# Hybrid decoder block: the gate projections as Strassen products, with sums of weights and tokens made in the first part

## The chip, the cores and the metric

The kernel runs on one core of a Trainium2 chip. The core has a matrix engine (TensorE, PE in the profile), three engines that work on tiles (VectorE or DVE, ScalarE or ACT, GpSimd or POOL), a queue engine that mainly issues transfers (SyncE, SP), and 16 DMA engines between DRAM and on-chip memory. Matmuls add up in PSUM banks of 128x512 float32. The metric is the device time of one execution in microseconds, the median of several runs.

## The reference, cut to what matters

```python
h = _rmsnorm(x, norm_pre_mix)              # x: (1, 2048, 1024)
proj = einsum('bsd,de->bse', h, w_in)
q, k, v = ...                              # 12 heads of 64, three dilations
u = gelu(proj[..., U0:Z0]); z = gelu(proj[..., Z0:GA0])   # 512 columns each
gate_a = sigmoid(proj[..., GA0:GB0])       # 1024 columns
gate_b = sigmoid(proj[..., GB0:IN_WIDTH])  # 1024 columns
y_attn = dilated attention of q, k, v
y_gmlp = u * (chunked spatial mix of layernorm(z))
merged = gate_a * (y_attn @ w_branch_attn) + gate_b * (y_gmlp @ w_branch_gmlp)
x = x + _rmsnorm(merged @ w_out)
h = _rmsnorm(x); x = x + _rmsnorm((relu(h @ w_mlp_in) ** 2) @ w_mlp_out)
```

The change concerns the products behind gate_a and gate_b: 2048 tokens by 1024 inputs by 2048 columns.

## The kernel before

Everything is float32, kept exact by splits: a number becomes a rounded high part and the rest as low part, and one product is three matmuls (high-high, high-low, low-high: `mm3`). `split_in` loads raw data, one engine makes the high part (L70 on ACT, L72 on POOL), another the low part by a subtraction (L78). Tokens are four chunks c of 512 in two halves (half 0: c = 0, 1). `hT[c]` is the normalised, transposed chunk, 8 slices of 128 inputs, both parts.

The program goes, for half 0 and then half 1, through v (`v_block`, eight blocks of 128 tokens) and q and k (`qk_pair`, twelve pairs per half: 48 matmuls, then DVE makes the rotation's products t, POOL joins them to r at L307 to L313, ACT and DVE split r into hl). Each half's weights wq come by `load_w`: 512 KB loads, high part on POOL, low part on DVE, three slots. While PE works on half 0, `keep_cols` also stores the transposed chunks 0 and 1 in DRAM (hT_d), because only two chunks fit on chip; chunks 2 and 3 stay on chip until the gates of half 1 are done, and `reload_h` brings 0 and 1 back one by one, high and low parts on POOL.

Then a generator, `filler`, works through u and z of half 1, the gates g of half 1 and half 0, and u and z of half 0. A step of it is one slice of one product, that is three matmuls. The attention is 48 units; between the pieces of a unit the program calls `steps(n)`, which puts n steps of the filler into PE's order, so that PE has work while ACT and DVE do the softmax. In PE's order of a unit there come: scores s, transposes pT of the previous unit's exponentials, products pv (from ph, a split made by ACT L688 and DVE L689, and pf, a copy by ACT L696), and transposes po of pvs (copied by ACT L704) whose reduction on DVE (L709) is the unit's output. Nine steps fall to a unit. After the units come `combine` (four chunks; att is stored, loaded back as A, weighted by DVE, and transposed to yt at L745, with fixed numbers of steps between) and the rest of the filler; then branches and gates are merged (from about 1104 us), and the MLP, which is itself made of Strassen products, follows.

The gates: 8 column blocks of 256 per half (w_g, `load_w`), each two column halves m by two chunks c by 8 slices: 96 matmuls. ACT copies each bank (gt) and SP stores it in gate_d. At sn == 6 of some of these products `sz_out` emits the spatial mixing of a z chunk.

PE's order is the order in which the program is written. ACT, DVE, POOL and SP are put in order by a scheduler, by its own model of when data will be there; on the chip each engine then runs its list strictly in that order, and an instruction that waits holds all behind it.

## Time and profile before

| what | value |
|---|---|
| runs | 2698.89, 2699.76, 2700.78 us; median 2699.76 |
| the profiled run | 2700.86 us, span 2698.8 us, granted clock 0.996 |
| v and qk, half 0 | 0 to 218 us |
| v and qk, half 1 | 218 to 425 us |
| u and z, half 1 | 425 to 514 us |
| gates of half 1 (hT_a), in the attention | 513.8 to 774.3 us |
| gates of half 0 (hT_b), attention and combine | 774.5 to 1013.6 us |
| u and z, half 0 | 1013.8 to 1104.2 us |

A profile row of instructions has line, engine, operation, tile names (out<-in), shapes and count, then busy time and the mean of one, then the time in which the engine sat idle before and what ended that. A row of the timeline has start and length in microseconds and, in brackets, the idle time before it. A row of a transfer has the tiles, the queue, count, KB each and the median time from issue to landing.

### The profile page before, as it was taken

How to read it: one execution, taken by the hardware profiler on the slowest of the kernel's cores; microseconds unless marked ns; L12 is line 12 of the kernel's file. 1: busy time of each engine (PE TensorE's matmuls, PEld its weight loads, DVE VectorE, ACT ScalarE, POOL GpSimd, SP SyncE). 2: the span in 40 equal slices, each digit the busy share in tenths (PEclk: the TensorE clock that was granted, in tenths of full speed). 3: DMA queues.
4: the chain of work that ended last, by engine and by line, in shares of the span. 5: the costliest groups of instructions: out<-in, count | busy, mean ns of one | idle time of the engine just before them, and what ended most of it. 6: DMA issues, size and time to landing. Idle time of an engine off the chain costs nothing. (4 is left out here: it accounts for less than half of the span.)

```text
span 2698.8 us, 34839 instructions
## 1 busy us (share of the span) xinstructions
PE 2663.4 (99%) x12674; PEld 2226.9 (83%) x12674; DVE 1582.5 (59%) x2677; ACT 1053.2 (39%) x2149; POOL 977.2 (36%) x837
## 2 busy tenths in 40 slices
PE   9999999999999999999899999999999999999998
PEld 8888888888888888888678888888888888888887
DVE  5665463334444345665456765555437888888866
ACT  5213111144444432344335555565545333333334
POOL 0351352210050004210413454323224776676645
PEclk9999999999999999999999999999999999999999
DMA  7445446266577846654656465554344212222236
GB/s 271 167 144 180 152 141 218 96 189 199 177 248 205 220 151 187 202 177 145 227 172 251 133 207 178 173 183 125 114 136 129 84 57 86 88 86 87 92 108 212
DMA packets 299197, 431.77 MB, mean 160 GB/s; under 512 B 52817, under 2 KB 166225, under 8 KB 299026
## 3 DMA queue, kind: packets, MB, share of 16 engines
q1 hardware_dynamic: 226864, 370.48, 43.5%
q10 hardware_dynamic: 64178, 32.06, 3.9%
q0 software_dynamic: 7984, 27.01, 2.6%
q8 instruction: 100, 1.64, 0.3%
q14 instruction: 71, 0.58, 0.1%
HBM read 286.67 MB, written 142.80 MB: 159 GB/s over the span
## 5 line engine op out<-in xcount | busy, mean ns | idle before, releaser
L1627 PE MATMUL ya<-T_spots,s 128*128 128x512 f32 x1176 | 289.4, 390 | 0.7 <-ACT T_spots L70 0.6
L1627 PEld LDWEIGHTS ya<-T_spots,s 128*128 128x128 f32 x1176 | 220.6, 188 | 47.4 <-ACT T_spots L70 1.0
L70 ACT ACTIVATE s<-sraw 128x768 fp32r<-128x768 f32 (+1 forms) x184 | 127.2, 696 | 330.4 <-POOL sraw L1428 155.7
L78 DVE TENSOR_TENSOR s<-sraw,s 128x512 fp32r<-128x512 f32 x172 | 184.1, 1095 | 8.6 <-ACT s L70 8.5
L1104 PE MATMUL aa<-B,A 128*128 128x512 f32 x768 | 182.3, 390 | 0.7 <-DVE A L85 0.7
L1104 PEld LDWEIGHTS aa<-B,A 128*128 128x128 f32 x768 | 143.9, 188 | 31.2 <-DVE A L85 1.1
L1627 PE MATMUL yc<-T_spots,s 128*128 128x512 f32 x624 | 159.7, 389 | 0.0
L72 POOL TENSOR_SCALAR w_g<-w_g_r 128x1024 fp32r<-128x1024 f32 x32 | 34.1, 1080 | 344.5 <-PE g L97 258.0
L1075 POOL TENSOR_TENSOR s<-w1r 128x512 f32<-128x512 f32 x32 | 42.3, 1322 | 309.3 <-DVE S L78 256.6
L95 PE MATMUL x<-hT_a,wq 128*128 128x512 f32 x384 | 149.8, 390 | 0.0
L96 PE MATMUL x<-hT_a,wq 128*128 128x512 f32 x384 | 149.5, 389 | 0.0
L97 PE MATMUL x<-hT_a,wq 128*128 128x512 f32 x384 | 149.5, 389 | 0.0
L709 DVE TENSOR_REDUCE o<-po 128x256 f32<-128x512 f32 x48 | 33.1, 690 | 184.3 <-PE po L708 184.3
L1627 PEld LDWEIGHTS yc<-T_spots,s 128*128 128x128 f32 x624 | 117.2, 188 | 24.3
L70 ACT ACTIVATE hl<-r 128x512 fp32r<-128x512 f32 x48 | 30.4, 632 | 238.1 <-POOL r L307 89.0
L95 PE MATMUL o<-wo,mg 128*128 128x512 f32 x256 | 102.1, 399 | 8.1 <-ACT mg L70 7.5
L78 POOL TENSOR_TENSOR T_spots<-w2r,T_spots 128x512 fp32r<-128x512 f32 x70 | 104.5, 1522 | 7.3 <-ACT T_spots L70 7.3
L95 PE MATMUL g<-hT_b,w_g 128*128 128x512 f32 x256 | 104.7, 409 | 0.0
L95 PE MATMUL g<-hT_a,w_g 128*128 128x512 f32 x256 | 104.3, 407 | 0.0
L78 DVE TENSOR_TENSOR A<-w1r,A 128x512 fp32r<-128x512 f32 x61 | 61.8, 1014 | 66.9 <-ACT A L70 66.9
L96 PE MATMUL o<-wo,mg 128*128 128x512 f32 x256 | 101.0, 394 | 0.0
L97 PE MATMUL o<-wo,mg 128*128 128x512 f32 x256 | 100.9, 394 | 0.0
(390 smaller groups left out, 7156.2 us busy)
## 6 DMA issues: line engine op xcount, KB each, us to landing
w1r<-in_w_mlp_in_dram SPq DMA_DIRECT2D x64, 512.0 KB, 3.8
sraw<-sd SPq DMA_DIRECT2D x128, 256.0 KB, 3.3
qk<-hl SPq DMA_DIRECT2D x24, 1024.0 KB, 5.1
qq<-qk SPq DMA_DIRECT2D x96, 256.0 KB, 4.9
w_g_r<-in_w_in_dram SPq DMA_DIRECT2D x32, 512.0 KB, 5.5
gated<-gt SPq DMA_DIRECT2D x64, 256.0 KB, 3.5
w2r<-in_w_mlp_out_dram SPq DMA_DIRECT2D x16, 1024.0 KB, 6.4
sd<-u ACTq DMA_DIRECT2D x63, 256.0 KB, 3.8
```

The source lines that it names most:

```text
L70: act.activation(hi, src, AF.Copy)
L72: pool.tensor_scalar(hi, src, 1.0, 1.0, op0=OP.mult, op1=OP.mult)
L78: (pool if lo_eng == "pool" else dve).tensor_sub(lo, src, f32(hi))
L95: pe.matmul(ps, lh, rh, start=start, stop=False)
L96: pe.matmul(ps, lh, rl, start=False, stop=False)
L97: pe.matmul(ps, ll, rh, start=False, stop=stop)
L709: dve.tensor_reduce(ot[:, :, j * 64:(j + 1) * 64], po.rearrange("p (b h e) -> p b e h", b=4, h=2), axis=AX.X, op=OP.add)
L1075: pool.tensor_add(s1, a21, a22)
L1104: pe.matmul(p, w[:, l, k, :], h[:, r, k, :], start=i in (1, 6, 5) and not k and not n, stop=k == 3 and n == 2, skip_group_check=True)
L1627: pe.matmul(p, s[:, l], w[r], start=i in (1, 2, 5) and not m and not o, stop=m == 1 and o == 2, skip_group_check=True)
```

## The change

Two neighbouring column halves (of 128) of a gate block, the two halves of the 1024 inputs and the two token chunks of a half form a 2x2 by 2x2 block product. Eight such pairs n per half are now done by Winograd's form of Strassen's scheme, seven products of 4 slices instead of eight: 12 matmuls each.

- In the first part, on POOL: `pre_s` (16 calls) loads a quarter of a block's weights and writes four sums of them to DRAM (sg_d, s1g_d); `pre_t` (16 calls) does the same for tokens (tg_d), whose four chunks are now all stored in hT_d by `keep_cols`. One call is written after each qk pair and after each v block of half 1; the scheduler is free in where it puts them.
- `gates()` takes the place of the 16 weight blocks. The products are grouped in phases: (1, 2), (6, 7), (5, 3), (4) for half 1, then the same for half 0; in a phase all eight n use the same one or two token operands. A product of one n is a piece: `piece` loads its weights (256 KB, rows of 512 bytes), `split_piece` splits them (POOL, DVE) into one of eight spots. The token operands of the next phase are loaded, as 512 KB loads, into opA or opB when the phase before has left it, and split by ACT and POOL (`operand`). Products of one n share banks and pass through 32 copies on ACT (L668, L670) and 80 additions on DVE (L673 to L684) into gx, gz and ga before the store.
- `reload_h` makes high parts on ACT instead of POOL. A unit of the attention has eight steps instead of nine, the combine's numbers of steps are 28, 18, 17, 19 instead of 33, 21, 20, 24, and u of half 0 runs chunk by chunk with both weight blocks held.

```diff
-            if c < 2:
-                raw = ...
+            raw = xp.tile([P, 4, P], F32, name=f"hr_{c}{i}{k}", tag="hr", bufs=3)
+            act.activation(raw, p3, AF.Copy)
+            sp.dma_start(hT_d[c, :, k:k + 4, i * P:(i + 1) * P], raw)
...
-            split_in(hT[c][:, :, k:k + 2], hT_d[c, :, k:k + 2, :], None, "pool", "pool")
+            split_in(hT[c][:, :, k:k + 2], hT_d[c, :, k:k + 2, :], None, "act", "pool")
...
+        def pre_t(half, k, j):
+            w = pre.tile([P, 5, 256], F32, name=f"pt{half}{k}{j}", tag="pre")
+            for c in range(2):
+                sp.dma_start(w[:, 2 * c:2 * c + 2], hT_d[2 * half + c][:, k::4, tsl])
+            b11, b21, b12, b22 = (w[:, n] for n in range(4))
+            pool.tensor_sub(b11, b12, b11)
+            pool.tensor_sub(b12, b22, b12)
+            pool.tensor_sub(b22, b22, b11)
+            pool.tensor_sub(b21, b21, b22)
+            pool.dma_start(tg_d[half][:, :, k, tsl], w[:, :4])
...
+        def pre_s(n, k):
+            sp.dma_start(both, a["w_in"][13 + n]...)
+            pool.tensor_add(s1, a21, a22)
+            pool.tensor_sub(a21, a11, a21)
+            pool.tensor_sub(a11, s1, a11)
+            pool.tensor_sub(a12, a12, a11)
+            pool.dma_start(sg_d[n]..., both)
+            pool.dma_start(s1g_d[n][:, k:k + 2], s1)
...
-    queue += [(13 + n, "g", n, 1) for n in range(8)] + [(13 + n, "g", n, 0) for n in range(8)]
+    queue += [(13, "g", 0, 1)]
...
+    PHASES = ((1, 2), (6, 7), (5, 3), (4,))
+    PIECES, SPLITS, LAST = 4, 3, 104
+    seq = [(half, i, n) for half in (1, 0) for ops in PHASES for i, n in lagged(ops)]
...
+    def operand(half, i, slot):
+        for k in range(0, 4, 2):
+            sp.dma_start(f32(slot)[:, 1, k:k + 2], src[i][:, k:k + 2])
...
+    def gates():
...
+        for t, (half, i, n) in enumerate(seq):
+            if t in starts:
...
+                    for j, i2 in enumerate(phases[ph + 1][1]):
+                        todo += operand(phases[ph + 1][0], i2, slots[s][:, j])
...
+            elif todo and (t % 2 == 0 or len(phases[ph][1]) == 1):
+                w, k = todo.pop(0)
+                split(w[:, 0, k:k + 2], w[:, 1, k:k + 2], f32(w)[:, 1, k:k + 2], "act", "pool")
+            piece(t + PIECES)
+            split_piece(t + SPLITS)
...
+            for k in range(4):
+                for m, (l, r) in enumerate(((0, 0), (0, 1), (1, 0))):
+                    pe.matmul(p, w[:, l, k], h[:, r, k], ...)
+                if t == 2 and late:
+                    sz_out(*late.pop(0))
+                yield
...
+            if i == 1:
+                act.activation(x, p, AF.Copy)
...
+            elif i == 6:
+                dve.tensor_add(z, x, p)
...
-    steps(6 if n > 1 else 9)
+    steps((6 if n < 4 else 5) if n > 1 else 9)
...
-        steps((33, 21, 20, 24)[n])
+        steps((28, 18, 17, 19)[n])
```

Three places in the engines' orders. The first is ACT in an attention unit. Before, each unit has the two ph, the exponentials e, pf and pvs, with a gate copy gt here and there:

```order
L688 ACTIVATE ph_4980<-pT_4975 128x512 [waits PE_49,Activation_49]
L663 ACTIVATE e_4946,o_4655<-e_4946,nm_4961 128x256 [waits DMAHW1_49,DVE_49]
L663 ACTIVATE e_4946,o_4655<-e_4946,nm_4961 128x256 x3
L688 ACTIVATE ph_4988<-pT_4983 128x256 [waits PE_49,Activation_49]
L696 ACTIVATE pf_4991<-pT_4983 128x256 [waits DVE_49]
L549 ACTIVATE gt_5008<-g_4933 128x512 [waits DMAHW6_49,PE_49]
L704 ACTIVATE pvs_5024<-pv_5015 128x512 [waits PE_49,Activation_49]
```

After (the names are the same; opB is the tile for token operands), at the end of the second phase:

```order
L833 ACTIVATE e_5521,o_5039<-e_5521,nm_5536 128x256 x3
L858 ACTIVATE ph_5563<-pT_5558 128x256 [waits PE_49,Activation_49]
L70 ACTIVATE opB<-opB 128x1024 [waits DMAHW1_49]
L866 ACTIVATE pf_5566<-pT_5558 128x256 [waits DVE_49]
L874 ACTIVATE pvs_5596<-pv_5587 128x512 [waits PE_49,Activation_49]
L70 ACTIVATE opB<-opB 128x1024 [waits DMAHW5_49]
```

PE's rows for the same stretch, after; g_5508 on its first row is the last product that reads the operand in opB's first half (g_5410 reads the second), and pf_5566 is used four rows on:

```order
L656 MATMUL g_5508<-opB,spots_4381 128x512 x3
L656 MATMUL g_5410<-opB,spots_4381 128x512 x12
L872 MATMUL pv_5587<-ph_5555,v_5038 128x256 x4
L872 MATMUL pv_5587<-ph_5563,v_5038 128x256 x2
L872 MATMUL pv_5587<-pf_5566,v_5038 128x128 x2
L656 MATMUL g_5508<-opB,spots_4381 128x512 x6
```

The two high parts of opB now stand ahead of pf_5566 and behind pvs_5596, each waiting for a transfer that the slot's last matmul lets go; ACT's list holds seven such places ahead of a pf.

The second is POOL in the first part. Before, the weights wq of the first qk pairs are its first work after the start:

```order
L72 TENSOR_SCALAR wq_941<-wq_r_942 128x1024
L72 TENSOR_SCALAR wq_941<-wq_r_946 128x1024
L72 TENSOR_SCALAR wq_952<-wq_r_953 128x1024
L72 TENSOR_SCALAR wq_952<-wq_r_957 128x1024
L72 TENSOR_SCALAR wq_1097<-wq_r_1098 128x1024
```

After (ps is the tile of a weight sum), the end of eleven calls of `pre_s`, which all stand ahead of the first wq:

```order
L442 DMA sgd<-ps_1755 256x1x512
L439 TENSOR_TENSOR ps_1858<-ps_1858 128x2x128
L443 DMA s1gd<-ps_1858 128x256
L440 TENSOR_TENSOR ps_1858<-ps_1858 128x2x128
L441 TENSOR_TENSOR ps_1858<-ps_1858 128x2x128
L442 DMA sgd<-ps_1858 256x1x512
L72 TENSOR_SCALAR wq_947<-wq_r_948 128x1024
L72 TENSOR_SCALAR wq_947<-wq_r_952 128x1024
L438 TENSOR_TENSOR ps_2087<-ps_2087 128x256
```

The high part of the first wq moved from the first place to the place behind eleven sums; one more weight sum and eight token sums follow at once.

The third is DVE at the turn from the last unit to the combine. Before, the last two reductions of po are followed by the low parts of w_u, and then by the combine's maximum M:

```order
L709 TENSOR_REDUCE o_8002<-po_8551 128x4x64 [waits PE_49]
L709 TENSOR_REDUCE o_8002<-po_8602 128x4x64 [waits PE_49]
L78 TENSOR_TENSOR w_u_8877<-w_u_r_8878,w_u_8877 128x1024 [waits DMAHW1_49,Pool_49]
L78 TENSOR_TENSOR w_u_8877<-w_u_r_8882,w_u_8877 128x1024 [waits DMAHW2_49,Pool_49]
L720 TENSOR_TENSOR M_8618<-A_8614 128x16 [waits DMAHW1_49,DMAHW0_49]
```

After (spots are the gate pieces, ga the adds of a gate's bank):

```order
L78 TENSOR_TENSOR spots_4165<-ga_4493,spots_4165 128x512 [waits DMAHW5_49,Pool_49]
L78 TENSOR_TENSOR w_u_9202<-w_u_r_9203,w_u_9202 128x1024 [waits DMAHW6_49,DMAHW3_49,DMAHW7_49,DMAHW1_49,Pool_49]
L879 TENSOR_REDUCE o_8413<-po_9048 128x4x64 [waits PE_49]
L684 TENSOR_TENSOR ga_4484<-ga_4484,g_9041 128x512 [waits PE_49]
L78 TENSOR_TENSOR w_u_9202<-w_u_r_9207,w_u_9202 128x1024 [waits DMAHW0_49,Pool_49]
```

The low part of the second w_u block moved ahead of the last reduction, and waits there for POOL's high part of it.

More of the change, by code (lines that the diff above doesn't have):

```diff
@@ L428, in block_kernel @@
                 v_block(rp, wv, c, i, between)
+                if half:
+                    next(pre_steps)()
                 if (c, i) == (0, 1):
@@ L521, in want, with lagged @@
             else:
-                loaded[q] = load_w(wi, f"w_{kind}{n}{half}", "pool" if (kind, half) == ("g", 0) and n == 2 else "dve")
+                loaded[q] = load_w(wi, f"w_{kind}{n}{half}")
+    PHASES = ((1, 2), (6, 7), (5, 3), (4,))
+    def lagged(ops):
+        first = [(n, (ops[0], n)) for n in range(8)]
+        return [z for _, z in sorted(first + [(n + 1.5, (i, n)) for n in range(8) for i in ops[1:]])]
+    PIECES, SPLITS, LAST = 4, 3, 104
+    seq = [(half, i, n) for half in (1, 0) for ops in PHASES for i, n in lagged(ops)]
@@ new lines, in block_kernel, with piece @@
+    g_ = dict(raw={}, w={}, b={})
+    def piece(t):
+        if t >= len(seq):
+            return
+        half, i, n = seq[t]
+        raws = g_["raws"]
+        r = raws[t % 4] if t < 8 else raws[4 + (t - LAST) % 5] if t >= LAST else raws[(t - 4) % 6]
+        if i < 3:
+            src = w_src(13 + n, i - 1)[:, :, :P]
+        elif i == 5:
+            src = s1g_d[n]
+        else:
+            kk, m = {6: (0, 0), 7: (0, 1), 3: (1, 0), 4: (1, 1)}[i]
+            src = sg_d[n][:, kk, :, m * P:(m + 1) * P]
+        sp.dma_start(r.rearrange("p (k c) -> p k c", k=4), src)
+        g_["raw"][t] = r
@@ L528, in filler @@
                 continue
+            if kind == "g":
+                yield from gates()
+                continue
             want(q)
-            want(q + 1)
-            if kind == "z" or (kind, n) == ("u", 1):
+            if queue[min(q + 1, len(queue) - 1)][1] != "g":
+                want(q + 1)
+            if (kind, n) == ("u", 1) or (kind, n, half) == ("u", 0, 0):
                 want(q + 2)
@@ L806, in block_kernel @@
     ec.close()
+    ega.close()
     e2r = ExitStack()
```

118 lines of the change are left out of this document (102 added, 16 removed).

## The prediction

> **What bounds the kernel now.** I read the page's totals first, then the windows by stage, then the rows of the gates, and last the timeline of one attention unit.
>
> ```profile
> span 2698.8 us, 34839 instructions
> PE 2663.4 (99%) x12674; PEld 2226.9 (83%) x12674; DVE 1582.5 (59%) x2677; ACT 1053.2 (39%) x2149; POOL 977.2 (36%) x837
> PEclk9999999999999999999999999999999999999999
> ...
> 87.00:218.00 131.00, 131.00 (x594) 108.80 (x593) 79.30 (x95) 17.01 (x29) 61.36 (x36) 1.00 0.53 166
> 514.00:720.00 206.00, 204.25 (x1167) 176.33 (x1166) 87.30 (x256) 85.49 (x252) 24.10 (x21) 1.00 0.64 196
> 720.00:940.00 220.00, 219.27 (x1250) 188.84 (x1249) 94.09 (x314) 94.75 (x297) 46.46 (x32) 1.00 0.76 214
> 940.00:1016.00 76.00, 76.00 (x393) 64.20 (x392) 30.32 (x109) 23.26 (x67) 8.10 (x9) 1.00 0.52 159
> ```
>
> A window row gives start and end, its length, then busy time and count of PE, PEld, DVE, ACT and POOL, the granted clock, the DMA share and GB/s. PE is busy for all but 35 us of 2698.8, at full clock in every slice. Two things therefore set the time: how many matmuls there are, and whether PE ever waits. Every removed matmul is a gain of one pitch; every microsecond in which PE must wait for another engine is a loss, because there is no idle PE time for it to vanish in. No other engine is above 45% in the stretch of the gates (514 to 1014), so it is late work, not too much work, that can hurt.
>
> **What is removed.** A row "a/b/c" gives shortest, median and longest ns.
>
> ```profile
> L95 PE MATMUL g<-hT_a,w_g x256: 388/390/487, 513.8 to 773.8; 128*128 128x512 f32 x128
> L97 PE MATMUL g<-hT_b,w_g x256: 388/391/398, 774.9 to 1013.6; 128*128 128x512 f32 x128
> ...
> L95 PE MATMUL x<-hT_a,wq 128*128 128x512 f32 x384 | 149.8, 390 | 0.0
> ...
> 142.69 4.27 POOL L309 TENSOR_TENSOR r<-t,t 128x512 f32<-128x512 f32 x2 [5.66 <-DVE t L304]
> 164.45 4.27 POOL L309 TENSOR_TENSOR r<-t,t 128x512 f32<-128x512 f32 x2 [3.93 <-DVE t L304]
> ```
>
> The gates are 2 x 3 x 256 = 1536 matmuls. After the change: 2 halves x 8 column blocks x 7 products x 4 slices x 3 terms = 1344, so 192 go. A matmul's 390 ns overlaps its neighbour's, so the price is the pitch: qk has 3 x 384 = 1152 matmuls in 24 pairs, 48 each; two pairs lie between the two POOL rows, 21.76 us / 96 = 0.2267 us. **192 x 0.2267 = 43.5 us gained**, if PE never waits.
>
> **Operands in the attention stage: the largest cost.** Each of the 12 token operands arrives as two 512 KB loads, is cut into its high part by ACT (128x1024) and its low part by POOL. The slot it goes to becomes free only when PE ends the last product of an earlier phase, and the scheduler has put the high parts into ACT's order between copies that PE awaits: seven times just ahead of pf. This is one unit now:
>
> ```profile
> 592.00 0.36 ACT L688 ACTIVATE ph<-pT 128x256 fp32r<-128x256 f32 x1
> 592.85 0.38 ACT L696 ACTIVATE pf<-pT 128x256 f32<-128x256 f32 x1 [0.49 <-DVE ph L689]
> 595.23 0.60 ACT L704 ACTIVATE pvs<-pv 128x512 f32<-128x512 f32 x1 [1.99 <-PE pv L702]
> ...
> 593.80 0.88 PE L702 MATMUL pv<-ph,v 128*128 128x256 f32 x6
> 594.52 0.61 PE L702 MATMUL pv<-pf,v 128*128 128x128 f32 x4
> 594.88 0.47 PE L95 MATMUL g<-hT_a,w_g 128*128 128x512 f32 x1
> 596.35 0.60 PE L708 MATMUL po<-ident,pvs 128*128 128x128 f32 x4
> ...
> w_g_r<-in_w_in_dram SPq DMA_DIRECT2D x32, 512.0 KB, 5.5
> sraw<-sd SPq DMA_DIRECT2D x128, 256.0 KB, 3.3
> T<-td SPq DMA_DIRECT2D x8, 512.0 KB, 5.0
> ...
> DMA to landing us min/median/max: 4.5/6.8/8.1
> ...
> L70 ACT ACTIVATE T<-T x8: 1042/1050/1066, 1751.5 to 1770.4; 128x1024 fp32r<-128x1024 f32 x8
> ```
>
> The landing row with three figures is that of hT_b<-hTd, 512 KB loads issued at 758 to 777, in the midst of the attention. Now pf ends at 593.23 and PE asks for it at 594.52: 1.3 us to spare. After the change, by PE's order, the slot comes free 12 gate matmuls and 6 pv matmuls ahead of pf's use: 12 x 0.2267 + 0.72 (593.80 to 594.52) = 3.4 us. In that time must fit the landing, the high part (1.05) and pf (0.38). With the landing of T<-td, 5.0, which has the same layout in DRAM and the same bytes, this takes 6.4, and PE waits 3.0 us. Bounds: 3.3 (sraw, half the bytes) gives 1.3, and 6.8 (hT_b) gives 4.8. Seven places: **21 us (9 to 34)**. Behind the waiting high part on ACT queue pf, pvs and the next unit's exps; PE waits for each in turn, but the gates between give later ones cover.
>
> The Trainium skill, "SBUF — State Buffer", section "The DMA setup-cost knee", fits a transfer as 2 us plus its bytes at 436 GB/s: an estimate of 3.2 us for 512 KB, by which these seven would cost 9 us instead of 21, and the sum below would come out near no change. The trace disagrees: its 512 KB rows are at 5.0 and above at the median, beside other traffic.
>
> The other high parts stand ahead of pvs. PE asks for pvs 1.47 us (594.88 to 596.35) after pv; the copy has 0.5 us to spare there, and a high part whose data are there takes 1.05, so five such places cost some 0.6 to 0.7 each, 3.5. At three more (the four parts for the third phase, one ahead of the exps of the last group, and the reload of hT ahead of a pvs) the load itself is late by PE's order; I price them as above, 3 x 3.0. **13 us together (4 with none late, 18 at 6.8).**
>
> **Pieces and evictions: nothing.** 112 weight pieces take POOL a high part and DVE a low part each, 80 adds go to DVE, and 32 of 64 copies leave ACT.
>
> ```profile
> L899 DVE TENSOR_TENSOR g<-g,b x58: 672/680/689, 1129.9 to 1410.1; 128x512 f32<-128x512 f32 x58
> L72 POOL TENSOR_SCALAR yt<-yt 128x512 fp32r<-128x512 f32 x6 | 4.0, 676 | 9.3 <-DMA yt<-yad 9.3
> L78 POOL TENSOR_TENSOR hT_b<-hT_b 128x1024 fp32r<-128x1024 f32 x8 | 19.2, 2395 | 0.7
> L78 DVE TENSOR_TENSOR hl<-r,hl x48: 673/694/1956, 104.5 to 430.7; 128x512 fp32r<-128x512 f32 x48
> ```
>
> A unit gets two pieces: DVE 2 x (0.68 + 0.69) = 2.7 us more per 9 us, less the w_g low parts, from 42% now (87.30 of 206) to some 65%. POOL 2 x 0.68 and, for an operand, 2 x 2.4. Splits run up to eight pieces ahead, which is the cover; a piece that is late by its whole landing would show as PE waiting on spots. Upper bound 8 us, that is one late piece (5.0 + 0.68 + 0.69 less the cover) here and there at phase ends; I take 0.
>
> **The turn from z to the gates.** The third sz step now comes 27 matmuls (6.1 us) after z, at about 519.7.
>
> ```profile
> 513.99 0.60 ACT L501 ACTIVATE z<-z 128x512 f32<-128x512 f32 x1 [8.43 <-PE z L97]
> 518.96 0.68 DVE L503 BATCH_NORM_STATS2 bs<-z 128x6 f32<-128x512 f32 x1
> 521.23 1.92 DVE L508 TENSOR_SCALAR z<-z,mv,r_ln 128x512 f32<-128x512 f32 x4
> ```
>
> The normalization takes 4.2 us from bs to the end of z (523.15). Four low parts of pieces now stand ahead of bs on DVE, each behind a POOL high part: 4 x 0.69 to 4 x 1.37 after 514.6, so bs starts at 517.4 to 520 and z ends at 521.6 to 524.3. **3.5 us (0 to 5).**
>
> **The combine.** Here the slack is read between DVE's last add and PE's transpose:
>
> ```profile
> 1007.68 1.23 DVE L740 TENSOR_TENSOR A<-A 128x1024 f32<-128x1024 f32 x1
> ...
> 1010.19 1.03 PE L745 MATMUL yt<-ident,A 128*128 128x128 f32 x8
> ```
>
> The add ends at 1008.91, PE comes at 1010.19: 1.3 us. With 28 steps instead of 33, PE comes 5 x 3 x 0.2267 = 3.4 us sooner: 2.1 us late. Ahead of the last reduction on DVE (and so of the store and reload of att) stands a w_u low part, which waits for POOL's high part behind as many as four low parts of 2.4 us. If half of that is past by then, 5 us; one of two w_z low parts inside the chain adds 1.2. **8 us (2 to 13).**
>
> **The sums in the first part.** POOL did next to nothing until wq at 81.9:
>
> ```profile
> 81.90 3.03 POOL L72 TENSOR_SCALAR wq<-wq_r 128x1024 fp32r<-128x1024 f32 x2 [80.01 <-PE va L97]
> 102.56 2.55 POOL L307 TENSOR_TENSOR r<-t,t 128x512 f32<-128x512 f32 x2 [1.95 <-DVE t L304]
> ...
> L95 PE MATMUL x<-hT_a,wq x19: 389/389/397, 87.2 to 99.5; 128*128 128x512 f32 x19
> ...
> L1427 POOL TENSOR_TENSOR sraw<-sraw 128x256 f32<-128x256 f32 x56 | 41.9, 748 | 161.7 <-DVE s L78 158.8 <-DVE s L85 3.0
> L980 POOL DMA_DIRECT2D td<-tq x32 | 17.7, 555 | 2.4 <-POOL tq L975 2.4
> hTd<-hr SPq DMA_DIRECT2D x16, 256.0 KB, 2.8
> ```
>
> Eleven weight sums now stand ahead of that wq on POOL. One is four 128x256 operations and two DMA issues: 4 x 0.75 + 2 x 0.56 = 4.1 us, and with three buffers load, work and store (5 + 4.1 + 2.8) / 3 = 4.0, the same. SP issues the loads behind the store of the fourth block, near 39 us; the first lands at 44, the eleventh sum ends at 44 + 45 = 89. High part 1.05 and DVE's low part 1.2 make 91.3 against 87.2: 4 us. Then qk: in POOL's order twelve more sums (eight of tokens, four operations and one issue, 3.6 us; four of weights) stand ahead of the r of the fourth pair. From 91, twelve sums (8 x 3.6 + 4 x 4.1 = 45), eight wq high parts (8.4) and eight r (8 x 1.3 = 10.4) end at 155. Now the first pair's r ends at 105.1, 17.9 us after x began. If r is late, t is not free, DVE cannot read the next pair's x, and PE stops one pair later, 10.9 us: the limit for the fourth pair is 91.2 + 3 x 10.9 + 17.9 + 10.9 = 152.7, so PE waits 2 us more, and 1 or 2 for DVE's low parts queued behind. The later pairs recover, since three sums follow them at most until the next v blocks. **8 us (0 to 18).** The 16 extra ACT copies and stores fall where ACT has 17 of 131 us: 0.
>
> **Sum:** -43.5 + 21 + 13 + 0 + 3.5 + 8 + 8 = +10. The profiled run took 2700.86 us; the median of the runs is 2699.76, 1.1 less. Forecast for the median: 2699.8 + 10 = **2710**.
>
> **Rivals.** (1) *The operands' waits are hidden.* If ACT makes up for a late high part while PE goes through the gates of the next unit, the two operand terms vanish: -43.5 + 3.5 + 8 + 8 = -24, 2676; with the other terms at their low ends as well, -41.5, 2658. If each wait merely shrinks to the 3.3 us landing, 9 + 3.5 + 3 x 1.3 = 16, the sum is -8, 2692; the skill's fit above would be this case. For it: PE waits only 2.5 us in 514 to 940 now, though ACT and DVE stand in one line there too. Against: a load cannot be issued before its slot is free, and 3.4 us later PE asks. It decides from a landing of about 2 us, or where pf has another 3 us of cover. Chance 0.30. (2) *DMA is full.* A piece is 512-byte rows, and the pieces and operands bring some 24 MB more into a stretch with shares of 0.64 and 0.76: landings of 6.8 and more, 34 + 18 + 19.5 - 43.5 = +28, 2728. Against: a quarter of the share is still unused. 0.14. (3) *POOL binds in the first part*: sums take 5 us each instead of 4, beside busy loads, and the term is 20 to 25: 2722 to 2727. 0.11. (4) *Losses and gain about cancel*: landings near 3.5, 2695 to 2705. 0.10. That the matmuls are not saved is excluded by PE's order, which holds 1344.
>
> **Numbers.** The forecast has 0.35. About 0.2% (5.4 us) is what a measurement here tells from no change. Slower: 0.35 + 0.14 + 0.11 = 0.60; within: 0.10; faster: 0.30. The range is 2670 to 2730: from below the middle of rival 1 to rival 2. The forecast's own range, its bounds half used, is 2702 to 2720.
>
> **What would show it.** Right: PE idle in the gate stretch by some 34 us, ended by ACT's pf or pvs, with ACT's own idle time before a high part of opA or opB ended by the load; landings of opB near 5. PE idle before x near 87 and some 50 us later, after POOL's sums; before sz near 520; before yt near 1010. PE busy some 43 us below 2663. Wrong: pf without stalls and PE idle below 40 us in all (then faster), or idle before g, ended by spots (then pieces are late, a term I put at nothing).

## The result, and the profile after

The change makes the kernel slower: 2778.98 us (median of 4 runs, 2775.52 to 2780.59) against 2699.75 (2698.89 to 2700.78), a ratio of 1.0293 with a 95% interval of 1.0278 to 1.0308. The forecast was 2710. The direction was right; the loss is 79 us instead of 10.

The page's totals after:

```profile
span 2778.8 us, 35465 instructions
PE 2652.3 (95%) x12482; PEld 2211.0 (80%) x12482; DVE 1713.7 (62%) x2839; ACT 1076.0 (39%) x2167; POOL 1193.2 (43%) x1107
PEclk9889999999999999999999999999999999999999
```

192 matmuls are gone (12674 to 12482), worth 43.5 us by the prediction's pitch, but PE is busy only 11 us less. PE's idle time went from 35 to 126 us, and the clock row shows eights at the start, where it was nine throughout.

Windows by stage show where it went. First the kernel before, then after: the first part, the gates, and u and z of half 0 (length, then PE busy and its count, PEld, DVE, ACT, POOL, granted clock, DMA share, GB/s).

```profile
0.00:422.00 422.00, 417.45 (x2089) 354.13 (x2090) 242.50 (x359) 101.21 (x216) 137.05 (x90) 1.00 0.53 176
...
514.00:1014.00 500.00, 497.52 (x2797) 427.71 (x2796) 210.66 (x676) 202.91 (x615) 76.66 (x58) 1.00 0.67 198
1014.00:1104.00 90.00, 90.00 (x409) 74.39 (x407) 42.27 (x96) 22.27 (x32) 39.30 (x30) 1.00 0.52 162
```

```profile
0.00:486.00 486.00, 433.68 (x2090) 363.99 (x2091) 262.20 (x359) 109.50 (x232) 271.35 (x266) 0.94 0.69 235
...
578.00:1076.00 498.00, 467.12 (x2597) 399.88 (x2596) 297.16 (x782) 210.28 (x608) 149.87 (x145) 0.97 0.80 235
1076.00:1186.00 110.00, 94.85 (x419) 77.97 (x418) 62.91 (x147) 29.81 (x41) 46.06 (x34) 0.94 0.61 198
```

A window's length less its busy time is PE's idle time. If as many matmuls take more busy time, the clock was lower. The window of the gates holds 200 matmuls fewer after, not 192, and that of u and z ten more, so some 2 us of the clock counted in the last stage belong to the gates.

| stage | length | idle, before to after | busy, before to after | what that says |
|---|---|---|---|---|
| first part | +64 | 4.6 to 52.3 | 417.5 to 433.7, same matmuls | 47.8 of waits, 16.2 of clock |
| u, z half 1 | 0 | 0 | 92 in both | nothing |
| gates | -2 | 2.5 to 30.9 | 497.5 to 467.1 | -43.5 of matmuls, +28.4 of waits, +13.1 of clock |
| u, z half 0 | +20 | 0 to 15.2 | 90 to 94.9 | 15.2 of waits, 4.9 of clock |
| rest | -2 | | | |

So 91 us of new waits and 34 us of lower clock stand against 43.5 us of matmuls, with 2 us the other way: +80 for the two profiled spans. PE's waits after (total, times, longest):

```profile
PE x L95 <- DVE t L305: 22.9, 4, 9.2
PE po L878 <- ACT pvs L874: 19.4, 7, 4.4
PE x L95 <- POOL wq L72: 17.3, 2, 15.7
PE yt L915 <- issue: 12.1, 1, 12.1
...
PE g L656 <- POOL spots L72: 4.6, 1, 4.6
...
PE pv L872 <- DVE ph L859: 3.2, 2, 1.6
...
PE g L656 <- ACT gx L668: 2.5, 1, 2.5
...
PE pv L872 <- ACT pf L866: 0.7, 2, 0.4
```

Two of the three largest are in the first part (x), where the prediction had 8 us for everything. The prediction's largest term, the seven waits for pf, is 0.7 us.

**The first part.** POOL's timeline (bracket: idle time before, and what ended it), then transfers (count, KB each, us to landing), then what the load queue SP itself waited for up to 230 us:

```profile
45.52 0.74 POOL L438 TENSOR_TENSOR ps<-ps 128x256 f32<-128x256 f32 x1 [43.63 <-DMA ps<-in_w_in_dram]
...
70.29 0.73 POOL L438 TENSOR_TENSOR ps<-ps 128x256 f32<-128x256 f32 x1 [5.91 <-DMA ps<-in_w_in_dram]
...
107.56 2.16 POOL L72 TENSOR_SCALAR wq<-wq_r 128x1024 fp32r<-128x1024 f32 x2
```

```profile
ps<-in_w_in_dram SPq DMA_DIRECT2D x16, 512.0 KB, 6.2
sgd<-ps POOLq DMA_DIRECT2D x16, 512.0 KB, 6.8
```

```profile
SPq L435 <- DMA sgd<-ps: 49.1, 10, 7.4
```

Eleven sums run from 45.52 to 107.56, 5.6 us each where 4.1 were reckoned. The loop over three buffers fits this: load 6.2, work about 4.3 (four operations and two issues), store 6.8, together 17.3, and a third of that is 5.8. The prediction had put the store at 2.8 us, from a row of 256 KB. SP stands in line for a buffer whose store has not landed, and POOL, in order, waits for the load. So the first wq comes at 107.56, not 89, and PE waits 15.7 us for it. Of these 18.5 us, 10.2 are the two waits for loads above, 6.7 are work (a sum takes POOL 4.7 us with its gaps, not 4.1), and 1.5 are the later start.

That the store is larger does not by itself explain the 6.8 us: in the kernel before, POOL stores other tiles of 512 KB (x1d) in 2.9. Traffic seems to have a part. Between 45 and 108 us the DMA share is 0.87, against 0.54 before, and hTd<-hr, the row that gave the price, goes from 2.7 us (40 to 220 us) to 7.4. In experiment 1, with a share of 0.69, hTd<-hr is back at 2.8, but sgd still takes 5.8: what else makes this store slow stays open.

**One late operand in the gates.** SP, ACT and PE around the end of a phase:

```profile
709.54 0.33 SPq L608 DMA_DIRECT2D opB<-tgd  x1
...
722.45 0.38 SPq L608 DMA_DIRECT2D opB<-tgd  x1
```

```profile
715.10 1.05 ACT L70 ACTIVATE opB<-opB 128x1024 fp32r<-128x1024 f32 x1
716.05 0.37 ACT L866 ACTIVATE pf<-pT 128x256 f32<-128x256 f32 x1
...
730.44 1.06 ACT L70 ACTIVATE opB<-opB 128x1024 fp32r<-128x1024 f32 x1 [3.86 <-DMA opB<-tgd]
731.40 0.58 ACT L874 ACTIVATE pvs<-pv 128x512 f32<-128x512 f32 x1
```

```profile
708.11 1.63 PE L656 MATMUL g<-opB,spots 128*128 128x512 f32 x6
...
716.68 0.61 PE L872 MATMUL pv<-pf,v 128*128 128x128 f32 x4
...
732.03 0.66 PE L878 MATMUL po<-ident,pvs 128*128 128x128 f32 x4 [3.29 <-ACT pvs L874]
```

The load ahead of this pf goes out 7.1 us before PE uses pf (709.54 to 716.68), not 3.4. A load writes two of the operand's four slices, and these were free when six matmuls of the slot's last product were through (708.11 to 709.5); its other six come after the scores and pT. ACT's high part at 715.10 follows its predecessor without idle time, so PE has no wait. The last of the four loads for opB, issued at 722.45, is late instead, at a pvs: its high part waits 3.86 us for the transfer, and PE 3.29 us for the pvs behind it.

### The profile page after: what moved, and what is told of

Its sections match the earlier page's. It is cut to its first block, busy times and chain, and to the rows that moved or that the text cites. A ratio compares the mean times of both kernels' runs of the same rounds, so it can differ in the third digit from the quotient of the medians.

```text
span 2778.8 us, 35465 instructions
## 1 busy us (share of the span) xinstructions
PE 2652.3 (95%) x12482; PEld 2211.0 (80%) x12482; DVE 1713.7 (62%) x2839; ACT 1076.0 (39%) x2167; POOL 1193.2 (43%) x1107
## 5 line engine op out<-in xcount | busy, mean ns | idle before, releaser
L95 PE MATMUL x<-hT_a,wq 128*128 128x512 f32 x384 | 155.1, 404 | 40.2 <-DVE t L305 22.9
L97 PE MATMUL x<-hT_a,wq 128*128 128x512 f32 x384 | 154.1, 401 | 4.6 <-DVE wq L78 4.6
L96 PE MATMUL x<-hT_a,wq 128*128 128x512 f32 x384 | 153.9, 401 | 0.0
L656 PE MATMUL g<-opB,spots 128*128 128x512 f32 x576 | 150.0, 404 | 0.0
L656 PE MATMUL g<-opA,spots 128*128 128x512 f32 x576 | 149.7, 402 | 0.0
L70 ACT ACTIVATE hl<-r 128x512 fp32r<-128x512 f32 x48 | 30.4, 632 | 271.7 <-POOL r L309 132.5
L72 POOL TENSOR_SCALAR spots<-gr 128x512 fp32r<-128x512 f32 x72 | 46.1, 643 | 206.7 <-PE g L656 173.5
L95 PEld LDWEIGHTS x<-hT_a,wq 128*128 128x128 f32 x384 | 75.1, 196 | 57.8 <-POOL wq L72 17.7
L656 PEld LDWEIGHTS g<-opB,spots 128*128 128x128 f32 x576 | 105.5, 192 | 19.0 <-DVE spots L78 0.4
L656 PEld LDWEIGHTS g<-opA,spots 128*128 128x128 f32 x576 | 104.0, 190 | 18.1
L1600 POOL TENSOR_TENSOR sraw<-sraw 128x256 f32<-128x256 f32 x56 | 41.8, 747 | 161.8 <-DVE s L78 158.8
L95 PE MATMUL o<-wo,mg 128*128 128x512 f32 x256 | 102.0, 398 | 8.0 <-ACT mg L70 6.3
```

The costliest lines, as they stand in the source:

```text
L70: act.activation(hi, src, AF.Copy)
L72: pool.tensor_scalar(hi, src, 1.0, 1.0, op0=OP.mult, op1=OP.mult)
L95: pe.matmul(ps, lh, rh, start=start, stop=False)
L96: pe.matmul(ps, lh, rl, start=False, stop=False)
L97: pe.matmul(ps, ll, rh, start=False, stop=stop)
L656: pe.matmul(p, w[:, l, k], h[:, r, k], start=i in (1, 6, 5, 4) and not k and not m, stop=k == 3 and m == 2, skip_group_check=True)
```

## The experiments

Each edit is to the changed kernel, unless it says otherwise. The kernel before ran beside each, with medians of 2697 to 2701 us.

**1. The sums behind the rotation (e1_spread).** Each sum is tied on POOL behind the r of the pair, or the work of the v block, that it is written after.

```diff
+        def next_sum():
+            last = next(i for i in reversed(nc.cur_bb.bb.instructions) if i.engine == mybir.EngineType.Pool)
+            with tc.issue_after(last):
+                next(pre_steps)()
...
-                    next(pre_steps)()
+                    next_sum()
```

> All 32 sums are made, with the same loads, operations and stores, but each is queued on POOL behind the r of the pair (or the work of the v block) after which it is written, one per pair, in place of fourteen ahead of the first r. Theory A (the place of the sums in POOL's list holds wq and r back): x starts again near 87 us, the last x ends within 8 us of the 422.0 of before, PE's waits for DVE t and POOL wq in the first part fall from 41 us to under 6, and the run takes 2778.98 - 56 to 64 = 2715 to 2723 us. Rival B (the sums' transfers crowd the DMA engines, shares of 0.87 and 0.80): the bytes are the same, so most of the 64 us stay: above 2750 us.

2742.77 us (2740.57 to 2744.96), ratio 1.0165 (1.0136 to 1.0195). 36 of the 79 us came back, not 56 or more, and more than the rival allowed. Half 0 is nearly as it was before the change (581 matmuls in the stretch, 594 before), and the loss has moved to the v blocks of half 1:

```profile
87.00:218.00 131.00, 129.74 (x581) 107.29 (x579) 97.49 (x89) 15.03 (x26) 107.99 (x97) 1.00 0.69 236
218.00:300.00 82.00, 63.62 (x345) 55.49 (x346) 35.29 (x56) 25.23 (x57) 44.86 (x55) 0.88 0.89 291
```

PE idles 18.4 of these 82 us, mostly waiting for ACT's copies hr (11.0 by PE's list of waits) and DVE's normalised tokens x (8.6), with DMA at 0.89. The order on POOL explains half 0. The second cost lies in the transfers or in their order on SP; this run does not tell the two apart.

**2. No sums at all (e2_raw).** The calls of `pre_s` and `pre_t` are left out, and the products that read sums read raw weights and tokens of the same sizes instead, so the gates' values are not computed.

```diff
-                next(pre_steps)()
+                pass
...
-            src[o] = tg_d[half][:, n]
+            src[o] = hT_d[c + n // 2][:, 4 * (n % 2):4 * (n % 2) + 4]
```

> The sums are left out altogether; products 3 to 7 read raw weights and chunks of tokens from DRAM in place of the sums, so their values are not the gates. The extra stores of chunks 2 and 3 stay. Theory A: the first part is as before within 3 us (last x near 422 to 425), the run takes about 2778.98 - 62 = 2717 us, the rest of it unchanged: gates near 498 us, u and z of half 0 near 110 us. A rival, that the extra copies on ACT and stores of chunks cost a good part of the 64 us: x would still end above 435 and the run would be above 2728 us.

2714.82 us (one run), close to the 2717 expected. The first part ends at 422.5 us, as in the kernel before: all 64 us are the sums' own. What remains above the kernel before, 17 us (this run's 2714.82 less 2698.11), is the gates and the half-0 stage.

**3. The high parts of wq on ACT (e3_wq_act).** This takes wq, but not r, from behind the sums on POOL.

```diff
-                nxt = load_w(0, f"wq00{half}")
+                nxt = load_w(0, f"wq00{half}", hi_eng="act")
```

> Only the high parts of wq go to ACT, so they no longer stand behind the sums; the sums stay where the scheduler puts them on POOL, ahead of the r. Theory A says both queues matter and POOL's list is as long less 24 us of wq: x starts near 90, but PE then waits for DVE t instead; 2755 to 2775 us. Rival C (the late wq alone is the loss, the r follow from it): the 20.5 us of waits at wq and their slow clock go, 2778.98 - 25 to 35 = 2744 to 2754 us or lower.

2760.28 us (one run), within the first theory's range: 19 us back. But x starts at 107, not near 90. PE still waits 16.0 us for t behind r, and 15.3 us for the wq, now made by ACT. ACT's rows show why:

```profile
105.54 0.60 ACT L202 ACTIVATE junk<-x 128x512 f32<-128x512 f32 x1 [14.10 <-DMA x<-in_x_dram]
...
106.17 1.99 ACT L70 ACTIVATE wq<-wq_r 128x1024 fp32r<-128x1024 f32 x2
```

ACT itself stands 14.1 us before wq, for tokens x whose load SP has not issued: they go out at 98.27 (98.46 in the change), behind sums' loads that wait for a buffer. The sums block the first qk pairs by two roads, POOL's order and SP's.

**4. Loads tied as well (e4_both).** As 1, with each sum's loads tied on SP behind the pair's last transfer.

```diff
+            for e in (mybir.EngineType.Pool, mybir.EngineType.SP):
+                es.enter_context(tc.issue_after(next(i for i in reversed(nc.cur_bb.bb.instructions) if i.engine == e)))
```

> As the run with the sums queued behind each pair's r, but their loads are queued behind that pair's last transfer on SP too, so that none waits on SP for a buffer. Theory A2 (what was left, 29 us in the v blocks of half 1, is SP: sum loads wait there for their buffers, behind them the stores of hr, behind those ACT's hr copies and PE's transposes): the last x ends at 422 to 430 instead of 451.4, no wait of PE for ACT hr or DVE x above 2 us, and the run takes 2743 - 21 to 29 = 2714 to 2722 us. Rival (the transfers crowd the DMA engines; share 0.89 in those v blocks): x still ends above 440 and the run above 2732.

2804.07 us (2803.53 to 2804.62), ratio 1.0391 (1.037 to 1.0411): wrong by more than 80 us. A load that goes out just ahead of its sum makes POOL wait for all of it, and r with it. POOL's waits from 87 to 486 us:

```profile
POOL ps L438 <- DMA ps<-in_w_in_dram: 111.6, 16, 11.0
POOL pt L425 <- DMA pt<-hTd: 37.3, 10, 9.4
```

Loads too early block SP (the change, 1); loads too late block POOL (4).

**5. Operands' high parts behind a pvs (e5_hi_late).** On top of 4: the high parts of opA, opB and of the reloads stand in ACT's list directly behind a pvs.

```diff
+    def release():
+        last = next(i for i in reversed(nc.cur_bb.bb.instructions) if i.engine == mybir.EngineType.Activation)
+        with tc.issue_after(last):
+            while held:
+                split(*held.pop(0))
...
-                split(w[:, 0, k:k + 2], w[:, 1, k:k + 2], f32(w)[:, 1, k:k + 2], "act", "pool")
+                held.append((w[:, 0, k:k + 2], w[:, 1, k:k + 2], f32(w)[:, 1, k:k + 2], "act", "pool"))
```

> As the run before, and the high parts of operands and of the reloaded hT are queued on ACT directly behind a pvs copy in place of ahead of one. Theory (PE's waits for pvs, 16 to 19 us in all, come from loads that have not landed when their high part's turn comes on ACT, and each wait lowers PE's clock after it): the waits for pvs fall below 3 us, and with the clock the run is 18 to 28 us shorter than the run before. Rival (it is ACT's load, not the place): the waits move to pf or ph, less than 8 us gained.

2783.43 us (2780.44 to 2786.42), 20.6 less than 4, as expected. The waits at pvs fell from 18.7 us in 4 to 2.1.

**6. The combine's chain first (e6_chain_first).** On top of 4: the low parts of the half-0 u and z weights are held behind the first chunk's chain on DVE.

```diff
+            if chain:
+                es.enter_context(tc.issue_after(chain[0]))
```

> As the run with both queues (not the one with late high parts), and the low parts of the second w_u block and of w_z are queued on DVE behind the combine's chain of the first chunk. Theory (the last reduction and the chain stood behind these low parts on DVE, 6.6 us and 2.4 us): the wait of PE at yt falls from 12 to 2 to 5 us and the run is 9 to 14 us shorter. Rival (att's store and reload alone set it): the wait at yt stays above 9 us; less than 4 us gained.

2806.95 us (2806.03 to 2807.87), nothing gained. The first wait at yt fell from 9.9 to 3.4 us, and the waits for A on POOL behind it rose from 2.7 to 11.9: the wait moved to the next chunk. The first part, which this edit does not touch, ended 4.6 us later in the profile (510.8 against 506.2), so a gain of 2 us could not be seen here.

**7. 5 and 6 together, with no other edit (e7_all).**

> Both of the last two edits. If the losses add up: 2714 to 2722 less 27 to 42, that is 2676 to 2692 us, below the 2698 to 2700 of the kernel before the change: the 43.5 us of the 192 matmuls would then show, less about 20 us of waits that stay. If they don't (the saved waits come back at spots): above 2700.

2789.25 us (2786.43 to 2794.0; ratio 1.0341, 1.0322 to 1.0361). The forecast was 2676 to 2692, missed by 100: it started from the 2714 to 2722 expected of 4, and 4 took 2804. The run settles nothing beyond 4 to 6.

**8. Loads two sums ahead (e8_prefetch).** As 1, with every load issued two sums before its work, and the high parts as in 5.

```diff
+            if not loaded_sums:
+                load_sum()
+                load_sum()
+            with tc.issue_after(last_on(mybir.EngineType.Pool)):
+                next(loaded_sums.pop(0))
+            load_sum()
```

> The sums one per pair behind its r, their loads two sums ahead of their operations (and behind the pair's last transfer on SP), and the late high parts of the attention. Theory (in the run with both queues POOL stood 145 us waiting for loads issued at the last moment, with r behind; with two sums of lead nobody waits): the last x ends at 422 to 435 us, POOL's waits for ps and pt loads in the first part stay under 25 us, and the run takes 2784 less 75 to 88 = 2696 to 2709 us. Rival (POOL or the DMA engines have no room for the sums whatever the order): the last x ends above 455, the run above 2728.

2706.21 us (8 runs, 2703.21 to 2711.21), ratio 1.0026 (1.0015 to 1.0038): the time is as expected. The first part ends at 439.1, a little behind the 435 expected at most, with 47 of the 64 us back. Beside it stand the gates of experiment 2, whose high parts are where the change has them:

```profile
514.00:1015.00 501.00, 469.38 (x2599) 401.67 (x2599) 297.78 (x783) 210.58 (x608) 148.63 (x145) 0.97 0.81 235
```

```profile
531.00:998.00 467.00, 455.02 (x2595) 391.12 (x2594) 288.57 (x782) 210.50 (x608) 149.11 (x145) 1.00 0.85 250
998.00:1109.00 111.00, 96.44 (x423) 79.17 (x422) 65.04 (x147) 29.96 (x42) 44.94 (x34) 0.92 0.62 198
```

The first row is experiment 2, the others this kernel. The gates are 34 us shorter for the same matmuls: 19.6 are idle time, and 14.4 are busy time, that is clock. Experiment 9, which makes the sums as here and leaves the high parts where the change has them, also takes 501 us for the gates, so ACT's order makes the difference, not the missing sums. With most of the waits gone (12.0 us of idle time are left), the gates take 33 us less than before the change: the seven products do bring most of their 43.5 us. All of it is given back in the first part (17) and in u and z of half 0 (21).

**9. The sums' order alone (e11_sums_only).** The tied sums and loads of 8 without the high parts of 5; there are no sums at the last two pairs of half 0, two each at the first and third pair of half 1, and the token sums start after ten weight sums instead of twelve.

```diff
-                next_sum()
+                if half or n < 5:
+                    next_sum()
+                if half and n < 2:
+                    next_sum()
```

> The change with one edit: the sums in a fixed order, one behind each pair's r, loads two sums ahead, none at the last two pairs of half 0 (where PE transposes chunk 2 and ACT's hl, waiting for a late r, stands ahead of its copies), two at the first and third d = 1 pairs of half 1 instead. Theory: of the 64 us lost in the first part some 50 to 60 come back, the last x ends at 424 to 436 us, the rest as in the change: 2719 to 2731 us. Rival (the DMA share of 0.96 in the v blocks of half 1 sets it): the last x ends at 439 or later as in the run before, above 2733 us.

2730.96 us (2726.68 and 2735.25), ratio 1.0111 (1.0093 to 1.013), at the upper edge. The first part ends at 436.1; PE waits 18.1 us at pvs. Half 1's v blocks still lose some 9 us.

**10. The combine's side work off its engines (e9_tail_act).** On top of 8: the half-0 u weights' high parts on ACT, the fourth chunk's additions on DVE.

```diff
-        eng = dve if c in (1, 2) else pool
+        eng = dve if c in (1, 2, 3) else pool
```

> As the run before, and at the end of the gates the high parts of w_u (half 0) are made by ACT in place of POOL and the combine's additions of chunk 3 by DVE in place of POOL. Theory (POOL's low parts of hT, four of 2.4 us, hold the second w_u's high part, that DVE's low part, that the last reduction): the waits at yt, 10.5 + 2.7 us, fall to 5 or less in all, and the run is 8 to 12 us shorter than the run before: 2686 to 2700. Rival (the store and reload of att and the chain itself set yt): less than 4 us shorter.

2703.94 us (7 runs, 2698.65 to 2708.52), ratio 1.0014 (1.0001 to 1.0027). 2.3 us below 8, the rival's case, and the two runs' ranges overlap. This is the lowest median of all versions, and it is no faster than the kernel before.

**11. All of these (e10_all).** 10 with the edits of 6 and of 9 added, and no other.

> The same order of the sums, the late high parts on ACT, w_u's high parts on ACT, the additions of chunk 3 on DVE, and the low parts of the second w_u and of w_z behind the first chunk's chain. Theory: first part 424 to 436, gates near 467 us (as in the two runs before, 32 of the 43.5 us saved), the waits at yt down from 13.3 to under 5: 2706 less 3 to 15 less 8 to 11, that is 2680 to 2695 us, faster than the kernel before by 0.2 to 0.7%. Rival (the wait at yt moves to the next chunk or to u's second weight block, and the first part stays): 2700 or above.

2706.61 us (10 runs), ratio 1.0024 (1.0015 to 1.0034): missed; the rival's time came. PE waits 14.9 us at yt ("issue", twice) and 4.5 for A. PE's rows at the first of them:

```profile
982.71 0.66 PE L930 MATMUL po<-ident,pvs 128*128 128x128 f32 x4
983.12 12.54 PE L708 MATMUL g<-opB,spots 128*128 128x512 f32 x54
...
1002.07 0.39 PE L97 MATMUL u<-hT_b,w_u 128*128 128x512 f32 x1
1010.40 1.94 PE L967 MATMUL yt<-ident,A 128*128 128x128 f32 x8 [7.93 <-issue]
```

The first yt comes 27.7 us after the last po. Before the change PE came to it 22.9 us after the last po (987.26 to 1010.19), with 33 steps between, and it was ready 1.3 us earlier. The combine's steps were cut from 98 to 82, that is from 66.7 to 55.8 us of cover at 0.68 us a step. Here the 28 steps (54 matmuls of the gates and 30 of u) cover up to 1002.5, and PE waits the other 7.9 us.

Fewer steps account for 2.1 us of this (five steps are 3.4 us, less the 1.3 to spare). The rest is the chain itself, which takes 27.7 us here and took 21.6 before. DVE shows where: the reduction of the last po starts 6.4 us after po began, where it took 0.6 before (987.89).

```profile
989.13 0.68 DVE L931 TENSOR_REDUCE o<-po 128x256 f32<-128x512 f32 x1
```

Ahead of it stand two low parts of spots, which take 2.9 us each (982.94 and 986.34), while POOL works on low parts of hT_b; in experiment 12, away from those, they take 0.69. No experiment was made to move these.

**12. More cover (e12_steps).** 11 with one step fewer in every third of the later attention units, and 33, 23, 21, 20 in the combine. The sums are moved once more: none at the last four pairs of half 0, two at each of the first four of half 1.

```diff
-            steps((6 if n < 4 else 5) if n > 1 else 9)
+            steps((6 if n < 4 else 4 if n % 3 == 0 else 5) if n > 1 else 9)
...
-        steps((28, 18, 17, 19)[n])
+        steps((33, 23, 21, 20)[n])
```

> The edits of e10_all with three numbers of the schedule changed: one step fewer of the filler in every third attention unit, so that more steps are left for the combine of half 0 (33, 23, 21 and 20 in place of 28, 18, 17 and 19), and two sums instead of one behind the first heads of half 1. Theory (the combine of half 0 is a chain of fixed length, and what the seven products took away was the work that covered it; the attention units have cover to spare): the waits at yt L930 fall from 19.4 us to under 6, the first part ends at 424 to 432 us (435 in e10_all), and the time is 2685 to 2694 us, faster than before. Rival (an attention unit needs its eight steps: with seven the PE waits at po and pv for the ACT, some 0.3 to 0.7 us in each of the units that lost one): what comes back at yt is lost in the units, and the time stays at 2700 us or above.

2708.54 us (5 runs, 2707.74 to 2713.55), ratio 1.0037 (1.0023 to 1.0051). The waits at yt fell from 19.4 to 6.1 us, near the theory's 6, and the time did not fall. The steps are not the only reason: the last reduction starts 1.4 us after its po began here. The first part did not move (436.8, 435.2 in 11). The rival's time came true, but not its cause: in the units PE has one longer wait, 5.2 us at a pvs. PE now reaches u before its operands are there, 11.7 us in six waits, of which these are two:

```profile
1004.18 0.79 PE L95 MATMUL u<-hT_b,w_u 128*128 128x512 f32 x1 [1.81 <-ACT hT_b L70]
...
1028.82 0.79 PE L97 MATMUL u<-hT_b,w_u 128*128 128x512 f32 x1 [4.56 <-DVE w_u L78]
```

**13. u's operands on the idle POOL (e13_pool_reload).** 12 with the high parts of the token reload, and both parts of the second u weight, on POOL.

```diff
-            held.append((w[:, 0], w[:, 1], f32(w)[:, 1], "act", "pool"))
+            held.append((w[:, 0], w[:, 1], f32(w)[:, 1], "act" if c else "pool", "pool"))
...
-                loaded[q] = load_w(wi, f"w_{kind}{n}{half}", hi_eng="pool" if half else "act")
+                loaded[q] = load_w(wi, f"w_{kind}{n}{half}", "pool" if not half and n else "dve",
+                                   hi_eng="pool" if half or n else "act")
```

> e12_steps with the high parts of the half-0 token reload hT_b0 and both parts of the second half-0 u weight on POOL, which stands idle from 988 to 1004 us there, in place of ACT and DVE, which stand in the combine's own chain. Theory (half 0 of u and z loses time only because its operands are formed on the engines on which the combine runs): the waits at u (11.7 us in e12_steps) fall under 4, the waits at yt stay under 7, the stage of u and z of half 0 gains 8 to 13 us, and the time is 2694 to 2701 us, the same as before. Rival (the operands come late because their loads and their buffers come late, not because of the engine): the waits at u stay above 8 us and the time at 2704 to 2710.

2712.37 us (5 runs), ratio 1.0053 (1.0039 to 1.0066): the rival, with a time above its 2704 to 2710. The waits at u are still 10.0 us and those at yt 9.9. SP and POOL show why: the reload's second pair of loads stands behind six loads of A, and POOL waits for it.

```profile
980.89 5.93 SPq L942 DMA_DIRECT2D A<-att  x6
986.87 2.06 SPq L239 DMA_DIRECT2D hT_b<-hTd  x2
```

```profile
995.41 3.67 POOL L72 TENSOR_SCALAR hT_b<-hT_b 128x1024 fp32r<-128x1024 f32 x1 [6.24 <-DMA hT_b<-hTd]
```

That the loads' place on SP is what limits 13 is read from these rows; putting the loads elsewhere was not tried.

## Why the prediction was wrong

**The matmuls: right.** 192 went, worth 43.5 us. In experiment 8, with most of the operands' waits gone, the gates take 467 us against 500, 33 of the 43.5 us.

**The sums in the first part: 8 us (0 to 18) predicted, 64 measured.** This is the step that failed. The mechanism was the prediction's own, and the third rival's (sums of 5 us, a term of 20 to 25): POOL's sums stand ahead of wq and r. Experiment 2 shows that all 64 us hang on the sums, 1 and 8 that most of it is their order and their loads. Its size went wrong in three places. The transfers were priced from other transfers in quieter stretches: the store at 2.8 us takes 6.8, the load at 5.0 takes 6.2. With POOL's own 4.7 us this makes a sum 5.6 us and the first wq 18.5 us later than reckoned. That the sums' loads would also hold SP, and tokens behind them, was in no term; experiment 3 shows it. "The later pairs recover" did not hold: there are four waits for t, of up to 9.2 us, at 165 and 199 us in half 0 and two more in half 1. And nothing was set down for the clock, 16.2 us of the 64.

**Operands: 21 us at pf and 13 elsewhere predicted.** The wait at pf is 0.7 us. At the place shown above the slot comes free slice by slice, earlier than "when PE ends the last product"; the other six were not followed in this way. The waits at pvs, ph and gx are 19.4, 3.2 and 2.5. Together with spots (4.6, priced at 0 with an upper bound of 8) this is 30.4 us against 37.5 for operands, pieces and the turn, where PE did not wait at sz at all: the total was close by luck, its places were not. Experiments 5 and 8 show that ACT's order makes the waits at pvs. The landings of opB were 6.2 us at the median, not 5.0, on the way to the second rival's 6.8. That the kernel's 512 KB rows are "at 5.0 and above" holds for the rows that the prediction shows only: in the same trace wq_r lands in 4.0, w1r in 3.8 and the stores x1d in 2.9.

**The combine: 8 us (2 to 13) predicted, 20 measured.** DVE's rows on the chain:

```profile
1068.43 2.05 DVE L78 TENSOR_TENSOR w_u<-w_u_r,w_u 128x1024 fp32r<-128x1024 f32 x1 [0.94 <-POOL w_u L72]
1070.41 0.68 DVE L879 TENSOR_REDUCE o<-po 128x256 f32<-128x512 f32 x1
...
1082.91 0.17 DVE L890 TENSOR_TENSOR M<-A 128x16 f32<-128x16 f32 x1 [7.70 <-DMA A<-att]
...
1084.90 1.22 DVE L78 TENSOR_TENSOR w_z<-w_z_r,w_z 128x1024 fp32r<-128x1024 f32 x1
```

The last po ends at 1063.5, and its reduction starts 6.9 us later behind two low parts of spots and one of w_u (5 were reckoned); two low parts of w_z stand in the chain (1084.90 and 1086.29), not one; and the reload of att takes 1.6 us longer than before. With the 2.1 us of the steps this makes up PE's wait of 12.1 us at the first yt. Its parts were named rightly and priced too low. The 3.0 us at the later chunks and up to 4.9 of clock were in no term. The prediction priced the cut of the steps only at the first chunk; over four chunks 16 steps of cover, 10.9 us, are gone. In 6, 10 and 11 moving side work brought little, but in 10 and 11 low parts of spots still stood ahead of the last reduction. 12 and 13 show that giving steps back brings out the next limit, the arrival of u's operands. What it would take to remove that one stays open.

**The clock: in no term, 34 us measured.** A wait of several microseconds costs more than its length. PE's rows of experiment 13, after a wait of 5.77 us (the duration of a matmul, by start):

```profile
1002.69 1.94 PE L970 MATMUL yt<-ident,A 128*128 128x128 f32 x8 [5.77 <-issue]
...
1006.99 0.63 PE L95 MATMUL u<-hT_b,w_u 128*128 128x512 f32 x1
1007.41 0.63 PE L96 MATMUL u<-hT_b,w_u 128*128 128x512 f32 x1
...
1009.14 0.39 PE L96 MATMUL u<-hT_b,w_u 128*128 128x512 f32 x1
1009.36 0.39 PE L97 MATMUL u<-hT_b,w_u 128*128 128x512 f32 x1
```

The pitch is 0.43 us until 1008.2, 5.5 us after the wait, and 0.23 later on. The Trainium skill, "TensorE: Matmul & The Clock Gate", section "Part 1: The HAM clock gate (the "warmup" mystery)", says that an idle window of about 3.4 us halves PE's clock and that a busy one of the same length restores it. The trace agrees in kind: the pitch is 0.43 against 0.23 us. In length it varies, 5.5 us of slow matmuls here and 3.0 after the wait of 7.9 us in experiment 11 (1010.40 to 1013.41), and in experiment 12 a wait of 2.7 us was already enough (1023.20 and 1023.63, 0.43 apart). That the waits lower the clock is borne out by experiment 8, where the gates have less of both. With 91 us of waits and 34 us of clock, each microsecond of waiting cost 0.37 more here. By that share the predicted 53.5 us of losses would have been about 73 (an estimate), and the forecast 2730.

**The chances.** "Slower" had 0.60, and the range ended at 2730. That the direction came true is in part luck, for the term that was to decide it, the waits at pf, did not come. The rival that applied, the sums, was weighed at 0.11 and taken alone; in the run it came together with the operands' waits, and more than twice as large as it was priced.

## What to carry to other kernels

A reduction of PE's work pays only if the work that prepares it fits on the other engines' and queues' lists; price a load-work-store loop with a wide bound where no row shows the same transfer in as busy a stretch (the same bytes are not enough: 2.9 us for one 512 KB store here, 6.8 for another), and check what stands behind it on the same queue. When filler work shrinks, ask what it was covering: a dependent chain behind it does not shrink with it, and here it grew. Price a PE wait of several microseconds at its length plus the slow matmuls that follow it.

## What was not expected of the hardware

A wait of 5.8 us cost PE 2.8 more behind it: eight transposes took 1.94 us instead of 1.03, and nine matmuls, from 1004.28 to 1008.21, 3.93 instead of 2.04. And the sums' loads on SP's in-order queue had a narrow optimum: free to go early, the loads of ps held SP for 49.1 us on buffers; tied to the last moment, the loads of ps and pt held POOL for 149 us; two ahead, 30 us (29.8 in the profile of experiment 8).
